# The last residual through TensorE, root and reciprocal on ScalarE and VectorE, and the last scale in three pieces, at the end of a one-core decoder layer

## The chip, the cores and the metric

The kernel runs on one core of a Trainium2 chip. The metric is the device time in microseconds (us). Names of engines: PE is TensorE, DVE is VectorE, ACT is ScalarE, POOL is GpSimd, SP is SyncE, which issues transfers. SBUF is the core's working memory of 128 partitions; PSUM is the memory into which PE writes its sums.

## The reference, cut to what matters

One decoder layer on 256 rows of width 1024, all in fp32. Two branches (block-sparse attention and gated linear attention) are merged by gates; the merged rows go through an output product, are added to the input, and a final normalisation follows:

```
merged = sigmoid(ga + b_merge[0]) * ya + sigmoid(gb + b_merge[1]) * yb
x = x + einsum('bsd,de->bse', merged, w_out)
return rms_norm(x, norm_f_g)

def rms_norm(x, g):
    y = x * rsqrt(mean(x * x, axis=-1) + 1e-6)
    return y * g
```

The change touches only the last two lines: the residual, the mean square, its inverse root, and the scale.

## The kernel before, in words

A number of fp32 precision is made of two numbers of PE's fast type, a high part and a low part, and each product is made of three matmuls: high by high, high by low, low by high (`three`). Weights come in chunks of 512 KB by transfers that SP issues (`load_to`); ACT makes the high part of a chunk (line 179), DVE the low part (line 180), both ahead of PE by a ring of five buffers (`split_to`, `prefetch`). Side work (attention, gates, merging) is written as generators that are stepped on between PE's matmuls by a modelled clock. Each engine works its instructions off in the order in which the code is written; an instruction waits for semaphores of what it reads, and all behind it on its engine wait with it.

The output product (`out_mm`) is the last use of PE. Rows are two tiles t = 0, 1 of 128. Tile 0 has two groups of 512 columns, tile 1 one of 512 and two of 256 (`cuts`); each group sums in a PSUM bank of its own (`po`). First all groups get the lower half of the inner dimension (`half` 0), then, in the order of tiles, the upper half. So the groups end one after the other: (0, 0), (0, 512), (1, 0), (1, 512), (1, 768), where the second number is the first column.

Behind each group stands its epilogue: line 859, DVE adds the input rows `xt` to the bank, into `y`; line 860, ACT squares `y` and sums along the row into a column of `fss` (the square writes a scratch tile, and a second small instruction reads the accumulator out); `scaled` (line 847), DVE multiplies `y` with the gain `nfb` into `yn`; lines 849 and 851, DVE adds the part sum to the mean square plus epsilon in the column `frs`. When a tile's last group is through, POOL raises `frs` to the power -0.5 (line 864), then DVE scales the upper 512 columns of `yn` (line 865) and ACT the lower 512 (line 866), and two transfers of 128 rows of 2 KB each go out: the upper half by SP's queue (line 867), the lower half by ACT's (line 868). In the trace `yn` and `nfb` carry the name `late`, the tile in which they lie, and the scratch tile is `junk`. After the last transfer has landed come the closing steps of the program.

Of the kernel before, what the change touches and what calls it, by code (L numbers as in the profile page):

```python
# [10 lines left out]
F32 = mybir.dt.float32  # L11
F32R = mybir.dt.float32r
BF16 = mybir.dt.bfloat16
I32 = mybir.dt.int32
AF = mybir.ActivationFunctionType
OP = mybir.AluOpType
# [3 lines left out]
P = 128  # L20
S = 256
NT = S // P
D = 1024
KD = D // P
H = 8
DH = 64
HP = H // 2
# [51 lines left out]
def layer(ctx, tc, x, norm_in_g, w_in, b_merge, w_fg2, b_fg, gla_g, w_pa, w_pb, w_out, norm_f_g,  # L79
          rope, causal, sums, masks, out):  # L80
    nc = tc.nc
    one = ctx.enter_context(tc.tile_pool(name="one", bufs=1))
# [7 lines left out]
    def mm(out, lhsT, rhs, start, stop):  # L90
        nc.tensor.matmul(out, lhsT, rhs, start=start, stop=stop)  # L91
        n = out.free_size() / 2400
        clock[0] += n if rhs.dtype == F32R else 4 * n
# [5 lines left out]
    def f32(ap):  # L99
        return ap.bitcast(F32)  # L100
# [4 lines left out]
    def bank(name, tag="acc", bufs=3):  # L105
        return psum.tile([P, 512], F32, name=name, tag=tag, bufs=bufs)

    def small(name):
        return bank(name, "small", 4)
# [73 lines left out]
    def prefetch(i):  # L183

        load_to(i + SPLIT + RAW - 2)
        split_to(i + SPLIT - 1)
# [3 lines left out]
    xt = one.tile([P, NT, D], F32, name="xt")  # L190
# [32 lines left out]
    ones = one.tile([P, P], F32, name="ones")  # L223
    nc.vector.memset(ones, 1.0)
    mhalf = one.tile([P, 4], F32, name="mhalf")
    nc.vector.memset(mhalf, -0.5)
    start = one.tile([P, 1], F32, name="start")
    nc.scalar.activation(start, mhalf[:, :1], AF.Sigmoid)
    ident = one.tile([P, P], F32, name="ident")
# [34 lines left out]
    junk = one.tile([P, D], F32, name="junk", tag="m0")  # L264
# [22 lines left out]
    ggz = one.tile([P, NT, 512], F32, name="ggz")  # L287
    gqT = one.tile([P, 2, S], F32, name="gqT")
    gkT = one.tile([P, 2, S], F32, name="gkT")
    oah = one.tile([P, HP, S], F32R, name="oah")  # L290
    oal = one.tile([P, HP, S], F32R, name="oal")
    obh = one.tile([P, GH, S], F32R, name="obh")
    obl = one.tile([P, GH, S], F32R, name="obl")
# [360 lines left out]
    def tick():  # L654
        step()
        ask = company["ask"]
        if ask and (sum(a[0] for a in ask) >= COMPANY or clock[0] - min(a[1] for a in ask) >= PATIENCE):
            company["open"] = True
            step()
            company["open"] = False  # L660
# [5 lines left out]
    def wait_for(*names):  # L666
        while not all(n in ready for n in names):
            wait(0.3)
# [50 lines left out]
    def three(o, ah, al, bh, bl, first, last):  # L719
        mm(o, ah, bh, start=first, stop=False)  # L720
        mm(o, ah, bl, start=False, stop=False)
        mm(o, al, bh, start=False, stop=last)

    for g in groups:
        ids, name = g["ids"], g["name"]
        if g["kind"] == "K":
            ps = [small(f"{name}{f}") for f in range(3)] + [bank(f"{name}3", "side", 1)]
            for i in ids:
                c = chunks[i]
                k = c["k0"]  # L730
# [13 lines left out]
        elif g["kind"] == "G":  # L744
            ps = {(t, b): (small if t and b else bank)(f"{name}{t}{b}") for t in range(NT) for b in range(2)}
            for i in ids:
                prefetch(i)
                c = chunks[i]
                for kk in range(c["nk"]):
                    k = c["k0"] + kk  # L750
# [8 lines left out]
        elif g["kind"] == "T":  # L759
            ps = [bank(f"{name}{t}") for t in range(NT)]  # L760
            for i in ids:
                prefetch(i)
                c = chunks[i]
                for kk in range(c["nk"]):
                    k = c["k0"] + kk
# [6 lines left out]
        elif g["kind"] == "F":  # L772
# [6 lines left out]
            if name == "gb0":  # L779
# [3 lines left out]
                nfb = late[:, 1, :D]  # L783
# [10 lines left out]
            for b in range(len(ids) // per):  # L794
                i = ids[b * per]
                ps = bank(name) if name != "gqk" else None
                if name == "gqk":
                    for _ in take("small"):
                        wait(0.3)
                    ps = small(name)  # L800
# [14 lines left out]


    def out_mm(ps, t, c0, c1, half):
        for k in range(4 * half, 4 * half + 4):
            c = chunks[oids[c0 // 512, k // 2]]
            ts = slice(t * P, (t + 1) * P)  # L820
            cs = slice(c0 % 512, c0 % 512 + c1 - c0)
            three(ps, merged[0][:, k, ts], merged[1][:, k, ts], c["hi"][:, k % 2, cs], c["lo"][:, k % 2, cs],
                  k == 0, k == KD - 1)

    y = one.tile([P, NT, D], F32, name="y", tag="m0")
    yn = late[:, 0].rearrange("p (t d) -> p t d", d=D)
    junk = work.tile([P, 512], F32, name="junk2", tag="t512", bufs=4)
    fss = one.tile([P, NT, 4], F32, name="fss")
    frs = one.tile([P, NT], F32, name="frs")
    cuts = {(0, 0): [(0, 512)], (0, 1): [(512, 1024)], (1, 0): [(0, 512)], (1, 1): [(512, 768), (768, 1024)]}  # L830
    po = {}
    for n in range(2):
        if n == 0:
            wait_for("m0", "m2")
        for t in range(NT):
            for c0, c1 in cuts[t, n]:
                for i in range(oids[n, 0], oids[n, 0] + 2):
                    prefetch(i)
                tick()
                b = len(po)  # L840
                po[t, c0] = (bank(f"po{b}") if b < 3 else small(f"po{b}"))[:, :c1 - c0]
                out_mm(po[t, c0], t, c0, c1, 0)
    prefetch(len(chunks))
    wait_for("m4", "m6")
    def scaled(t, j, part):
        cs = slice(*part)
        nc.vector.tensor_mul(yn[:, t, cs], y[:, t, cs], nfb[:, cs])
        if j == 0:
            nc.vector.tensor_scalar(frs[:, t:t + 1], fss[:, t, :1], 1.0 / D, EPS, op0=OP.mult, op1=OP.add)
        else:  # L850
            nc.vector.scalar_tensor_tensor(frs[:, t:t + 1], fss[:, t, j:j + 1], 1.0 / D, frs[:, t:t + 1],
                                           op0=OP.mult, op1=OP.add)

    for t in range(NT):
        parts = cuts[t, 0] + cuts[t, 1]
        for j, (c0, c1) in enumerate(parts):
            out_mm(po[t, c0], t, c0, c1, 1)
            cs = slice(c0, c1)
            nc.vector.tensor_add(y[:, t, cs], po[t, c0], xt[:, t, cs])
            nc.scalar.activation(junk[:, :c1 - c0], y[:, t, cs], AF.Square, accum_out=fss[:, t, j:j + 1])  # L860
            if j:
                scaled(t, j - 1, parts[j - 1])
        scaled(t, len(parts) - 1, parts[-1])
        nc.gpsimd.tensor_tensor(frs[:, t:t + 1], frs[:, t:t + 1], mhalf[:, :1], op=OP.pow)
        nc.vector.tensor_scalar(yn[:, t, 512:], yn[:, t, 512:], frs[:, t:t + 1], None, op0=OP.mult)
        nc.scalar.activation(yn[:, t, :512], yn[:, t, :512], AF.Copy, scale=frs[:, t:t + 1])
        nc.sync.dma_start(out[t * P:(t + 1) * P, 512:], yn[:, t, 512:])
        nc.scalar.dma_start(out[t * P:(t + 1) * P, :512], yn[:, t, :512])


_INS = ["x", "norm_in_g", "w_in", "b_merge", "w_gla_fg2", "b_gla_fg", "gla_norm_g", "w_proj_a", "w_proj_b",
# [29 lines left out]
```

## Time and profile before

| | |
|---|---|
| time, median of three runs | 211.7 us (210.26, 211.94, 211.7) |
| the profiled execution | 209.73 us, its span 208.0 us, granted clock of PE 0.997 |
| PE busy | 198.8 us, 96% of the span, 1683 matmuls |
| DVE, ACT, POOL busy | 141.6 (68%), 122.6 (59%), 32.5 (16%) us |
| chain that ended last | PE 67%, DVE 11%, ACT 11%, issue 5%, DMA 2% |

The span runs from the first to the last instruction; the time takes in what lies around it. A share of busy time is a mean over stages; what bounds a stage is read from its timeline and from the chain of work that ended last. PE's matmuls are pipelined, and their recorded lengths overlap.

### The profile page before, as it was taken

The numbers are of one execution on the slowest core, as the hardware profiler recorded it, in microseconds if no ns is written. First come the engines' busy times: TensorE is split into PE (matmuls) and PEld (weight loads), VectorE is DVE, ScalarE is ACT, GpSimd is POOL, SyncE is SP. The second block draws the span as 40 slices with busy tenths as digits, with TensorE's granted clock in tenths as the row PEclk, the third lists the DMA queues.
The fourth block names the chain that finished last, engine by engine and source line by source line (L and its number), as shares of the span: only waits on it lengthen the run. The fifth ranks groups of instructions, "written<-read, shape, count | busy, mean of one in ns | idle before, by whom it ended". The sixth has DMA issues, their size and how long they took to land.

```text
span 208.0 us, 4231 instructions
## 1 busy us (share of the span) xinstructions
PE 198.8 (96%) x1683; PEld 182.4 (88%) x1683; DVE 141.6 (68%) x261; ACT 122.6 (59%) x205; POOL 32.5 (16%) x31
## 2 busy tenths in 40 slices
PE   7999999999999999998999999999999999999970
PEld 2899999899999988775789999999999999989870
DVE  1566778969545899989765556945393959755371
ACT  4369927871999984156775629846455554552251
POOL 2000025800214540103000000200010060420011
PEclk9999999999999999999999999999999999999998
DMA  5999896594364456660343563966344584600022
GB/s 144 349 379 323 238 310 211 135 296 149 101 199 117 145 158 191 193 218 14 107 123 86 182 193 114 294 210 198 108 151 154 168 301 135 204 4 2 0 101 101
DMA packets 28501, 35.39 MB, mean 170 GB/s; under 512 B 1305, under 2 KB 21442, under 8 KB 28482
## 3 DMA queue, kind: packets, MB, share of 16 engines
q1 hardware_dynamic: 28178, 34.60, 54.1%
q10 hardware_dynamic: 304, 0.53, 0.7%
q8 instruction: 13, 0.21, 0.4%
q14 instruction: 6, 0.05, 0.1%
HBM read 34.08 MB, written 1.05 MB: 169 GB/s over the span
## 4 chain that ended last, share of the span: by engine, by line
PE 67%; DVE 11%; ACT 11%; issue 5%; DMA 2%; SPq 1%; POOLq 0%; POOL 0%; ACTq 0%; DVEq 0%
PE ga L91 11%; PE gb L91 11%; PE po L91 8%; PE gg L91 6%; PE gqk L91 6%; PE pa L91 5%; PE pb L91 5%; DVE lo L180 4%; ACT hi L179 4%; PE mg L91 3%; ACT z L700 3%; PE mq L91 3%; DMA xt<-in_x_dram 2%; PE gv L91 2%; DVE EX L417 2%
## 5 line engine op out<-in xcount | busy, mean ns | idle before, releaser
L180 DVE TENSOR_TENSOR lo<-raw,hi 128x1024 fp32r<-128x1024 f32 (+1 forms) x56 | 70.4, 1269 | 23.5 <-ACT hi L179 23.5
L179 ACT CAST hi<-raw 128x1024 fp32r<-128x1024 f32 (+1 forms) x56 | 57.7, 1048 | 21.5 <-PE po L91 6.0
L91 PE MATMUL ga<-xh,hi 128*128 128x256 f32 x64 | 18.1, 283 | 0.0
L91 PE MATMUL gb<-xh,hi 128*128 128x256 f32 x64 | 18.1, 282 | 0.0
L91 PE MATMUL gb<-xh,lo 128*128 128x256 f32 x64 | 17.9, 279 | 0.0
L91 PE MATMUL gb<-xl,hi 128*128 128x256 f32 x64 | 17.9, 279 | 0.0
L91 PE MATMUL ga<-xh,lo 128*128 128x256 f32 x64 | 17.8, 278 | 0.0
L91 PE MATMUL ga<-xl,hi 128*128 128x256 f32 x64 | 17.8, 278 | 0.0
L91 PE MATMUL po<-hi,ml 128*128 128x512 f32 (+1 forms) x40 | 13.9, 347 | 0.0
L91 PE MATMUL po<-lo,mh 128*128 128x512 f32 (+1 forms) x40 | 13.8, 346 | 0.0
L91 PE MATMUL po<-hi,mh 128*128 128x512 f32 (+1 forms) x40 | 13.7, 343 | 0.0
L91 PEld LDWEIGHTS ga<-xh,hi 128*128 128x128 f32 x64 | 12.1, 189 | 0.5 <-issue 0.5
L558 ACT ACTIVATE sm<-sm,mx 128x128 f32<-128x128 f32 (+1 forms) x16 | 7.1, 444 | 8.7 <-DVE mx L553 8.6
L91 PEld LDWEIGHTS gb<-xh,lo 128*128 128x128 f32 x64 | 12.1, 189 | 0.0
L91 PEld LDWEIGHTS gb<-xh,hi 128*128 128x128 f32 x64 | 12.1, 189 | 0.0
L91 PEld LDWEIGHTS ga<-xl,hi 128*128 128x128 f32 x64 | 12.0, 188 | 0.0
L91 PEld LDWEIGHTS gb<-xl,hi 128*128 128x128 f32 x64 | 12.0, 188 | 0.0
L91 PEld LDWEIGHTS ga<-xh,lo 128*128 128x128 f32 x64 | 12.0, 188 | 0.0
L511 POOL TENSOR_TENSOR s<-s,mhalf 128x4 f32<-128x4 f32 x2 | 2.3, 1172 | 54.6 <-DVE s L510 54.6
L624 POOL TENSOR_TENSOR m<-m,sa 128x512 f32<-128x512 f32 x4 | 7.0, 1743 | 23.9 <-DVE m L622 22.0
L91 PE MATMUL mg<-xh,hi 128*128 128x256 f32 x32 | 10.3, 321 | 0.0
L91 PE MATMUL mg<-xl,hi 128*128 128x256 f32 x32 | 9.5, 296 | 0.0
(197 smaller groups left out, 605.7 us busy)
## 6 DMA issues: line engine op xcount, KB each, us to landing
raw<-in_w_in_dram SPq DMA_DIRECT2D x36, 512.0 KB, 3.7
raw<-in_w_out_dram SPq DMA_DIRECT2D x8, 512.0 KB, 4.8
raw<-in_w_in_dram SPq DMA_DIRECT2D x4, 528.0 KB, 6.0
first<-in_w_in_dram SPq DMA_DIRECT2D x8, 256.0 KB, 5.5
raw<-in_w_proj_a_dram SPq DMA_DIRECT2D x4, 512.0 KB, 3.5
raw<-in_w_proj_b_dram SPq DMA_DIRECT2D x4, 512.0 KB, 4.4
xt<-in_x_dram SPq DMA_DIRECT2D x3, 256.0 KB, 5.7
late<-in_norm_f_g_dram SPq DMA_DIRECT2D x1, 512.0 KB, 5.0
```

Of the source, the lines that this page charges most:

```text
L91: nc.tensor.matmul(out, lhsT, rhs, start=start, stop=stop)
L179: nc.scalar.copy(c["hi"], raw)
L180: nc.vector.tensor_sub(c["lo"], raw, f32(c["hi"]))
L417: nc.vector.tensor_mul(e, e, halves(src, LEVELS[l], which))
L511: nc.gpsimd.tensor_tensor(s4, s4, mhalf, op=OP.pow)
L558: nc.scalar.activation(sm[i][:, cs], sm[i][:, cs], AF.Exp, bias=mx[:, i, t:t + 1], scale=0.125, accum_out=den[:, i, t:t + 1])
L624: nc.gpsimd.tensor_add(m, m, cut(sg["ga"]))
L700: nc.scalar.copy(z[i:i + 32], p2[i ^ 32:(i ^ 32) + 32])
```

## The change

The last group, (1, 768), gets its input rows on PE: an identity matrix, and high and low part of `xt` of these columns, are written by DVE into a tile `resid` (which takes the place of a tile whose use is over), and two matmuls with the identity as weights start the group's sum in PSUM. Its square and its scale read the bank itself. The mean square of all groups but the last is kept in `frs`; the last part sum, that column as a bias and the root are one ACT instruction, followed by a reciprocal on DVE. A square root of a column of ones stands ahead of the epilogues. The last scale of a tile is in three pieces: ACT the columns 0 to 255, DVE 768 to 1023 and then 256 to 767; for group (1, 768) the multiplication with the gain and the scale are one DVE instruction. Three transfers go out per tile in place of two, of 128, 128 and 256 KB. Of the memory layout, `part` and an unused tile `gap2` move the tiles allotted after them by 128 bytes per partition.

```diff
     def out_mm(ps, t, c0, c1, half):
+        add = (t, c0) == last
+        if add and not half:
+            mm(ps, resid[:, :P], resid[:, P:3 * P], start=True, stop=False)
+            mm(ps, resid[:, :P], resid[:, 3 * P:], start=False, stop=False)
...
-                  k == 0, k == KD - 1)
+                  k == 0 and not add, k == KD - 1)
...
+    last = (1, 768)
+    resid = one.tile([P, 5 * P], F32R, name="resid", tag="oah")
+    nc.vector.tensor_copy(resid[:, :P], ident)
+    nc.vector.tensor_copy(resid[:, P:3 * P], xt[:, 1, 768:])
+    nc.vector.tensor_sub(resid[:, 3 * P:], xt[:, 1, 768:], f32(resid[:, P:3 * P]))
...
+    part = one.tile([P, NT], F32, name="part")
+    one.tile([P, 24], F32, name="gap2")
+    nc.scalar.activation(start, ones[:, :1], AF.Sqrt)
...
-            nc.vector.tensor_add(y[:, t, cs], po[t, c0], xt[:, t, cs])
-            nc.scalar.activation(junk[:, :c1 - c0], y[:, t, cs], AF.Square, accum_out=fss[:, t, j:j + 1])
+            if (t, c0) == last:
+                z = po[t, c0]
+            else:
+                z = y[:, t, cs]
+                nc.vector.tensor_add(z, po[t, c0], xt[:, t, cs])
+            nc.scalar.activation(junk[:, :c1 - c0], z, AF.Square, accum_out=fss[:, t, j:j + 1])
             if j:
-                scaled(t, j - 1, parts[j - 1])
-        scaled(t, len(parts) - 1, parts[-1])
-        nc.gpsimd.tensor_tensor(frs[:, t:t + 1], frs[:, t:t + 1], mhalf[:, :1], op=OP.pow)
-        nc.vector.tensor_scalar(yn[:, t, 512:], yn[:, t, 512:], frs[:, t:t + 1], None, op0=OP.mult)
-        nc.scalar.activation(yn[:, t, :512], yn[:, t, :512], AF.Copy, scale=frs[:, t:t + 1])
-        nc.sync.dma_start(out[t * P:(t + 1) * P, 512:], yn[:, t, 512:])
-        nc.scalar.dma_start(out[t * P:(t + 1) * P, :512], yn[:, t, :512])
+                mean(t, j - 1)
+            if j == len(parts) - 1:
+                nc.scalar.activation(part[:, t:t + 1], fss[:, t, j:j + 1], AF.Sqrt, bias=frs[:, t:t + 1],
+                                     scale=1.0 / D)
+            if (t, c0) != last:
+                nc.vector.tensor_mul(yn[:, t, cs], z, nfb[:, cs])
+        r = frs[:, t:t + 1]
+        nc.vector.reciprocal(r, part[:, t:t + 1])
+        nc.scalar.activation(yn[:, t, :CUT], yn[:, t, :CUT], AF.Copy, scale=r)
+        for c0, c1 in ((768, D), (CUT, 768)):
+            if (t, c0) == last:
+                nc.vector.scalar_tensor_tensor(yn[:, t, c0:c1], z, r, nfb[:, c0:c1], op0=OP.mult, op1=OP.mult)
+            else:
+                nc.vector.tensor_scalar(yn[:, t, c0:c1], yn[:, t, c0:c1], r, None, op0=OP.mult)
+            nc.sync.dma_start(out[t * P:(t + 1) * P, c0:c1], yn[:, t, c0:c1])
+        nc.scalar.dma_start(out[t * P:(t + 1) * P, :CUT], yn[:, t, :CUT])
```

`CUT` is 256; `mean` holds the two statements that stood in `scaled` behind its multiplication.

The end of DVE's program before, from the add of the last group on (`po_2375` is its bank):

```order
L859 TENSOR_TENSOR y<-po_2375,xt 128x256
L847 TENSOR_TENSOR late<-y,late 128x256
L851 SCALAR_TENSOR_TENSOR frs<-fss,frs 128x1
L847 TENSOR_TENSOR late<-y,late 128x256
L851 SCALAR_TENSOR_TENSOR frs<-fss,frs 128x1
L865 TENSOR_SCALAR late<-late,frs 128x512
```

And of the change, from the add of the group before it on (`po_2379` is now the bank of the last group):

```order
L877 TENSOR_TENSOR y<-po_2366,xt 128x256
L862 TENSOR_SCALAR frs<-fss 128x1
L885 TENSOR_TENSOR late<-y,late 128x256
L864 SCALAR_TENSOR_TENSOR frs<-fss,frs 128x1
L887 RECIPROCAL frs<-part 128x1
L891 SCALAR_TENSOR_TENSOR late<-po_2379,frs,late 128x256
L893 TENSOR_SCALAR late<-late,frs 128x512
```

The add of the last group and its multiplication with the gain are gone; the reciprocal and the fused scale stand behind the last use of `fss`.

The end of ACT's program before, from the transfer of tile 0 on:

```order
L868 DMA out_dram<-late 128x512
L860 ACTIVATE junk_2295,fss<-y 128x512
L860 ACTIVATE junk_2295,fss<-y 128x256 x2
L866 ACTIVATE late<-late,frs 128x512
L868 DMA out_dram<-late 128x512
```

And of the change, from the same place on:

```order
L895 DMA out_dram<-late 128x256
L878 ACTIVATE junk_2295,fss<-y 128x512
L878 ACTIVATE junk_2295,fss<-y 128x256
L878 ACTIVATE junk_2295,fss<-po_2379 128x256
L882 ACTIVATE part<-fss,frs 128x1
L888 ACTIVATE late<-late,frs 128x256
L895 DMA out_dram<-late 128x256
```

The last square reads the bank, and the root stands between it and ACT's scale, which is half as wide.

## Rows read from the trace of the kernel before

**Rows 1.** Chain that ended last: start us, length us, what, how many.
```profile
174.34 5.44 PE pb L91 x48
179.78 16.47 PE po L91 x84
```
**Rows 2.** Timeline, PE's last matmul: start us, length us, engine, line, operation, shapes.
```profile
201.43 0.28 PE L91 MATMUL po<-hi,ml 128*128 128x256 f32 x1
```
**Rows 3.** Timeline behind it; in brackets idle time before and its releaser; q: queue.
```profile
201.74 0.42 DVE L859 TENSOR_TENSOR y<-po,xt 128x256 f32<-128x256 f32 x1 [0.28 <-PE po L91]
202.08 0.41 DVE L847 TENSOR_TENSOR late<-y,late 128x256 f32<-128x256 f32 x1
202.26 0.42 ACT L860 ACTIVATE junk<-y 128x256 f32<-128x256 f32 x1 [0.84 <-DVE y L859]
...
202.58 0.19 ACT L860 ACTIVATION_READ_ACCUMULATOR junk<-y 128x1 f32 x1
202.82 0.15 DVE L851 SCALAR_TENSOR_TENSOR frs<-fss,frs 128x1 f32<-128x1 f32 x1
203.05 0.56 POOL L864 TENSOR_TENSOR frs<-frs,mhalf 128x1 f32<-128x1 f32 x1 [4.11 <-DVE frs L851]
203.64 0.72 ACT L866 ACTIVATE late<-late,frs 128x512 f32<-128x512 f32 x1 [0.87 <-POOL frs L864]
203.65 0.49 DVE L865 TENSOR_SCALAR late<-late,frs 128x512 f32<-128x512 f32 x1 [0.67 <-POOL frs L864]
204.16 0.36 SPq L867 DMA_DIRECT2D out_dram<-late  x1
204.40 0.34 ACTq L868 DMA_DIRECT2D out_dram<-late  x1
```
**Rows 4.** Windows: stretch, us, busy by engine (count), PE clock, DMA share, GB/s.
```profile
204.16:205.00 0.84, 0.00 (x0) 0.00 (x0) 0.00 (x0) 0.21 (x1) 0.00 (x0) 1.00 0.00 0
205.00:206.40 1.40, 0.00 (x0) 0.00 (x0) 0.00 (x0) 0.00 (x0) 0.00 (x0) 1.00 0.99 370
```
**Rows 5.** Transfers: target, queue, count, KB each, median us from issue to landing.
```profile
out_dram<-late SPq DMA_DIRECT2D x2, 256.0 KB, 2.1
out_dram<-late ACTq DMA_DIRECT2D x2, 256.0 KB, 2.5
```
**Rows 6.** Timeline, idle stretches of DVE and ACT ahead of the epilogues.
```profile
185.02 1.23 DVE L180 TENSOR_TENSOR lo<-raw,hi 128x1024 fp32r<-128x1024 f32 x1 [2.40 <-ACT hi L179]
...
194.25 0.63 ACT L860 ACTIVATE junk<-y 128x512 f32<-128x512 f32 x1 [3.10 <-DVE y L859]
```
**Rows 7.** Groups of instructions: line, engine, form, count; busy us, mean ns; idle before.
```profile
L386 ACT ACT_TABLE_LOAD x1 | 1.3, 1283 | 0.0
L507 ACT ACTIVATE sq<-o 128x512 f32<-128x512 f32 x2 | 1.2, 598 | 5.9 <-PE o L91 5.9
L228 ACT ACTIVATE start<-mhalf 128x1 f32<-128x1 f32 x1 | 0.2, 202 | 0.0
L257 DVE SCALAR_TENSOR_TENSOR xl<-xp,vecs,xh 128x256 fp32r<-128x256 f32 x8 | 3.9, 482 | 3.4 <-ACT xh L256 3.4
```
**Rows 8.** Timeline, tile 0's last square and tile 1's first two adds.
```profile
197.06 0.63 ACT L860 ACTIVATE junk<-y 128x512 f32<-128x512 f32 x1 [2.08 <-DVE y L859]
...
199.37 0.68 DVE L859 TENSOR_TENSOR y<-po,xt 128x512 f32<-128x512 f32 x1
...
200.38 0.42 DVE L859 TENSOR_TENSOR y<-po,xt 128x256 f32<-128x256 f32 x1 [0.32 <-PE po L91]
```
**Rows 9.** Timeline of DVE, a reciprocal and the scale that reads it.
```profile
91.15 0.17 DVE L562 RECIPROCAL den<-den 128x2 f32<-128x2 f32 x1 [0.31 <-ACT sm L558]
91.36 0.28 DVE L564 TENSOR_SCALAR sm<-sm,den 128x128 f32<-128x128 f32 x1
```
**Rows 10.** Windows, a stretch with weight loads in rows of 1 KB.
```profile
145.00:150.00 5.00, 5.00 (x47) 5.00 (x46) 1.41 (x2) 2.44 (x4) 0.00 (x0) 1.00 0.47 149
```
**Rows 11.** GB/s in 40 equal slices of the span; the first weights' transfers.
```profile
GB/s 144 349 379 323 238 310 211 135 296 149 101 199 117 145 158 191 193 218 14 107 123 86 182 193 114 294 210 198 108 151 154 168 301 135 204 4 2 0 101 101
...
first<-in_w_in_dram SPq DMA_DIRECT2D x8, 256.0 KB, 5.5
```

More of the change, by code (lines that the diff above doesn't have):

```diff
@@ L289, in layer @@
     gkT = one.tile([P, 2, S], F32, name="gkT")
-    oah = one.tile([P, HP, S], F32R, name="oah")
+    oah = one.tile([P, HP, S], F32R, name="oah", tag="oah")
     oal = one.tile([P, HP, S], F32R, name="oal")
@@ L844, in layer, with mean @@
     wait_for("m4", "m6")
-    def scaled(t, j, part):
-        cs = slice(*part)
-        nc.vector.tensor_mul(yn[:, t, cs], y[:, t, cs], nfb[:, cs])
+    part = one.tile([P, NT], F32, name="part")
+    one.tile([P, 24], F32, name="gap2")
+    nc.scalar.activation(start, ones[:, :1], AF.Sqrt)
+    def mean(t, j):
         if j == 0:
@@ L852, in scaled @@
                                            op0=OP.mult, op1=OP.add)
+    CUT = 256
     for t in range(NT):
```

## Prediction

> **What bounds the kernel now.** First I read the chain that ended last. Nearly all of it is TensorE (PE): the output product alone stands in it as one unbroken piece of 84 matmuls, 16.47 us [rows 1]. So PE sets the time up to its last instruction, and no work that another engine does beside it is worth anything. Then I read the timeline behind the last matmul. The last of them starts at 201.43 and lasts 0.28 us [rows 2]; VectorE (DVE) takes up PE's result at 201.74. From here no PE is left, and one step follows the other [rows 3]: residual add on DVE (201.74), square with sum on ScalarE (ACT, 202.26), reading of its accumulator (202.58, done at 202.77), two small DVE steps of which the second (202.82) adds the last part sum, the power on GpSimd (POOL, 203.05, 0.56 us long), then the last scale, half on ACT and half on DVE (203.64), and two output transfers of 256 KB, issued by SyncE's queue at 204.16 and by ACT's at 204.40. Between the result of PE and the two issues lie 2.42 and 2.66 us.
>
> The windows behind the issues say what the transfers wait for [rows 4]: up to 205.00 no byte moves, from 205.00 to 206.40 the sixteen DMA engines are full (share 0.99, 370 GB/s). 370 GB/s over 1.40 us is 518,000 bytes, all but 1% of the 512 KB. The two transfers thus share one full pipe: its end is set by when the first of them was issued (204.16 + 0.84 = 205.00) and by the bytes, as long as the second arrives before the first has drained. They land 2.1 and 2.5 us after issue [rows 5], the second at 206.9; 1.1 us of closing steps follow to the end of the span at 208.0. The profiled execution took 209.73 us, 1.73 more than its span. The three timed runs lie at 210.26 to 211.94 with median 211.7; the profiled one is thus 0.9% below the median, and I carry the difference that I work out over to the median.
>
> **The change part by part.**
>
> *Residual through PE.* Two matmuls of 128x256 are added, ahead of the end of PE's queue, and PE is the bound: 48 of this size took 5.44 us [rows 1], 0.113 each, so all behind comes 0.23 us later. If they did not overlap as their neighbours do, it would be 2 x 0.28 = 0.56 [rows 2]. I take 0.23, since they are of the same type and width as their neighbours. Gone is the DVE add: from 201.74 to the square at 202.26 are 0.52 us [rows 3].
>
> *The preparation of the residual* is three DVE instructions (two casts, one subtraction), put ahead of weight splits (the low parts of the last weights). Each is no wider than the add of 128x256, 0.42 us [rows 3]; together at most 1.3 us. DVE stood idle for 2.40 us before the split at 185.02 [rows 6], and PE's unbroken piece runs past that, so the delay ends there and I cost it at nothing; without that idle time a weight split would come 1.3 us later.
>
> *The root's table.* A table load (1283 ns for those in the trace [rows 7]) and a square root of one column are put on ACT where it sat idle for 3.10 us, up to 194.25 [rows 6]: 1.28 + 0.2 fits, so nothing. The order of instructions has no further load behind it.
>
> *The new path behind PE* (PE's result now at 201.74 + 0.23 = 201.97):
> - square directly from PSUM: the accumulator was read 0.32 after the square began [rows 3]; ACT's square out of PSUM took 0.60 us where that out of SBUF took 0.63 [rows 7, 8], so 0.30 (at most 0.33). Reading 0.19: 202.46.
> - root with the sum of the earlier parts as its bias: it waits for its own engine. DVE's reciprocal and the scale that reads it start 0.21 apart at a length of 0.17 [rows 9], so such a wait costs 0.04. The root itself: no row. The nearest is the one-column activation with 202 ns [rows 7]; a column operand adds about 0.09, as the 0.72 us of the scale against the 0.63 of the square show [rows 3, 8]. I take 0.29, with 0.20 as the lower end: 202.79.
> - hand over to DVE 0.05 (202.77 to 202.82 [rows 3]), reciprocal and its wait 0.21 [rows 9]: 203.05. In place of this stood the add of the part sum, the pass to POOL, 0.56 us of power and the pass back, 202.77 to 203.64 = 0.87 [rows 3]. The new way from 202.46 to 203.05 takes 0.59.
> - DVE's fused scale of 256 columns out of PSUM: 482 ns for this form [rows 7], between 0.42 (the add) and 0.50: 203.53, issued on SyncE's queue 0.02 later at **203.55**. The scale of the other 512 columns starts 0.40 after it (0.08 of overlap, as between DVE's instructions before), takes 0.49 [rows 3]: 203.94, issue at **203.96**; the queue is free by then (an issue takes 0.36).
> - ACT's scale of 256 columns in place of 512: starts with DVE's at 203.05, 0.42 + 0.09 = 0.51, issue at **203.60**.
>
> *The transfers.* Three in place of two, same bytes. First byte 0.84 after the first issue, 204.39; the two pieces of 128 KB last 0.70 at 370 GB/s, to 205.09; the third can start at 203.96 + 0.84 = 204.80, so the pipe never runs dry and all ends at 204.39 + 1.40 = 205.79, against 206.40. That is **0.61 us** earlier, which is just the shift of the first issue (204.16 to 203.55). If instead the last transfer's own duration counts, the shift of the last issue decides: 204.40 - 203.96 = 0.44. The trace has the pipe at 0.99 share and both transfers of a tile inside one stretch, so I take 0.61.
>
> The Trainium skill puts this otherwise: its page "DMA: Bandwidth & Descriptors", section "Anatomy of one DMA", fits each DMA as about 2.0 us plus bytes over 436 GB/s, and the section "Measured" tells to batch to 1 MiB or more, which speaks against cutting 512 KB in three. By that fit a piece of 256 KB takes 2.6 us by itself (an estimate), and the gain would be 0.44. The trace has 2.1 and 2.5 for two that run together, so the fixed part is there, but it overlaps.
>
> *Tile 0's tail* gets the same edits and lies beside PE's matmuls of tile 1. Its square starts at 197.06 [rows 8], now 0.23 later: accumulator 197.83 to 198.02, root done at 198.35, reciprocal and wait 198.61, two scales at most 0.40 apart each: 199.41, when the add of tile 1 can start. It started at 199.37, and the next add waited 0.32 for PE [rows 8]: 0.04 late, hidden. The part sum that the last root needs as bias is ready some 0.1 to 0.3 us before its square begins; the root itself comes 0.5 later.
>
> **Sum.** 209.73 - 0.61 = 209.12 for an execution like the profiled one; 211.7 - 0.61 = **211.1** for the median. By the ends of the terms: earlier by 0.15 (root at 0.20, fused scale at 0.42) gives 0.76; later (0.33 more on PE, 0.03 on the square, 0.02 on the fused scale) gives 0.23.
>
> **Rivals.**
> - *The pieces give it back.* Rows of 1 KB in place of 2 KB could move more slowly. A stretch that loads weights in rows of 1 KB moved 149 GB/s at a share of 0.47, 317 per full pipe [rows 10]. At that rate for 256 KB the pipe lasts 0.12 longer; at half the rate 0.70 longer, and the gain is gone: 211.7. Against it: the pipe here is limited by its engines, and rows of 1 KB filled them at 86% of the rate.
> - *Slower: the transfers of one queue follow one another.* SyncE's queue now has two of the last three. If the second started only when the first had landed, the issue at 203.55 lands at 205.65, and 2.1 later, at 207.75, the other: 0.85 later than 206.9, so 212.5. It decides as soon as a wait of more than 0.6 us stands between the two. Against it: the first weights, in transfers of 256 KB on this same queue, took 5.5 us each to land, 48 GB/s if one had followed the other, and the second and third of the 40 slices of that time moved 349 and 379 GB/s [rows 11].
> - *The change does nothing for the end*, because the exit (1.1 us of closing steps) waits for something else. Against it: the second landing, at 206.9 [rows 5], is the last thing that any engine but the exit shows. It would give 211.7.
> - *More than worked out:* the pass over POOL costs more in other executions than the 0.87 us of the profiled one. No row tells; 1 us more of it gives 210.1.
>
> **How the numbers follow.** Forecast (0.2 to 0.8 us gained): 0.68. Pieces or exit take it back, within 0.2 of before: 0.18. One queue serial, or another new wait in the tail: 0.06. More than 0.8 gained: 0.08. The forecast's own range is 210.9 to 211.5. The timed runs spread over 1.68 us, though, and a median of a few of them moves by about half of that whatever the kernel, so the range goes on both sides beyond that: 209.7 is a gain of 0.8 taken from 210.5, which lies a third of the way up among the four times of the kernel before (209.73 to 211.94), and 212.0 is the gain gone and 0.3 of spread. About 1% (2.1 us) is what a measurement of this kernel can tell from no change. No case reaches 1% by its mechanism: faster takes the spread and the gain together, 0.07; slower the serial queue and the spread, 0.03; within, 0.90.
>
> **What would show it.** In the profile after: PE's last matmul about 0.23 later; ACT's last square starting directly behind PE, no add; root, reciprocal and fused scale inside 1.6 us; three issues near 203.55, 203.60 and 203.96; DMA full from 204.4 to 205.8; span near 207.4. Wrong if the table load stands in the tail, if the DMA windows show a gap or a lower rate at full share, if a split of weights now holds PE near 185 to 195, or if the closing 1.1 us grow.

## The result, and the profile after

The changed kernel takes 211.14 us (median of 20 runs, 210.44 to 213.11), the kernel before 209.79 us in runs between them on the same chip (20 runs, 209.12 to 212.03). The ratio is 1.0061, with a 95% interval of [1.0041, 1.0081]: **0.6% or 1.3 us slower, where 0.3% faster was forecast.** The three runs that the forecast started from had their median 1.9 us above that of the 20, so that the forecast of 211.1 lies beside the measured 211.14 by accident. What counts is the difference, and it has the other sign.

The profiled execution took 211.15 us, its span is 209.4 us; before it was 209.73 and 208.0. The 1.4 us are split by one moment, the start of PE's last matmul:

| | before | after | difference | forecast |
|---|---|---|---|---|
| start of PE's last matmul, us | 201.43 | 203.66 | +2.23 | +0.23 |
| from there to the end of the span, us | 6.53 | 5.71 | -0.82 | -0.84 |
| span, us | 207.96 | 209.37 | +1.41 | -0.61 |

The end behind PE went nearly as worked out, 0.82 less against 0.84. The two added matmuls take some of it back: with the 0.23 of the forecast 0.59 are gained, with the 0.3 that they cost in the runs below 0.5, against 0.61. But PE came to its end 2.0 us later than two more matmuls explain.

The timeline of after behind PE's last matmul (start us, length us, engine, line, operation; in brackets the idle time before and its releaser; q is a queue), which answers to [rows 2, 3]:

```profile
203.66 0.28 PE L91 MATMUL po<-hi,ml 128*128 128x256 f32 x1
...
204.03 0.38 ACT L878 ACTIVATE junk<-po 128x256 f32<-128x256 f32 x1 [0.39 <-PE po L91]
204.31 0.19 ACT L878 ACTIVATION_READ_ACCUMULATOR junk<-po 128x1 f32 x1
204.54 0.29 ACT L882 ACTIVATE part<-fss,frs 128x1 f32<-128x1 f32 x1
204.87 0.16 DVE L887 RECIPROCAL frs<-part 128x1 f32<-128x1 f32 x1 [1.03 <-ACT part L882]
205.06 0.51 ACT L888 ACTIVATE late<-late,frs 128x256 f32<-128x256 f32 x1 [0.23 <-DVE frs L887]
205.07 0.48 DVE L891 SCALAR_TENSOR_TENSOR late<-po,frs,late 128x256 f32<-128x256 f32 x1
205.47 0.48 DVE L893 TENSOR_SCALAR late<-late,frs 128x512 f32<-128x512 f32 x1
205.58 0.33 SPq L894 DMA_DIRECT2D out_dram<-late  x1
205.60 0.35 ACTq L895 DMA_DIRECT2D out_dram<-late  x1
```

Each step stands where the forecast had put it, counted from the last matmul: the square directly behind PE, root, reciprocal and fused scale, the first issue on SyncE's queue at 205.58, 1.92 behind the matmul (forecast: 203.55 - 201.66 = 1.89). The windows behind that issue (stretch, us, busy time by engine and count, PE's clock, DMA share, GB/s) answer to [rows 4], and the transfers (queue, count, KB, median us from issue to landing) to [rows 5]:

```profile
205.58:206.42 0.84, 0.00 (x0) 0.00 (x0) 0.36 (x1) 0.00 (x0) 0.00 (x0) 1.00 0.01 5
206.42:207.82 1.40, 0.00 (x0) 0.00 (x0) 0.00 (x0) 0.00 (x0) 0.00 (x0) 0.71 1.01 358
```
```profile
out_dram<-late SPq DMA_DIRECT2D x2, 256.0 KB, 2.4
...
out_dram<-late SPq DMA_DIRECT2D x2, 128.0 KB, 1.9
out_dram<-late ACTq DMA_DIRECT2D x2, 128.0 KB, 2.2
```

0.84 us without bytes, then 1.40 us of full DMA engines, as before. At about the same share three transfers move 358 GB/s where two moved 370: the lower rate at full share that the prediction named as a sign against it is there, but it is 3%, and from the first issue to the end of the span it is 3.79 us as against 3.80 before.

So the loss lies ahead. The chain that ended last in after (start us, length us, what, how many) answers to [rows 1]:

```profile
158.78 5.66 PE pa L91 x48
164.44 5.65 PE pb L91 x48
...
181.39 22.56 PE po L91 x122
```

48 matmuls of `pb` take 5.65 us where the same product took 5.44. The windows over the four stretches of `pa` and `pb`, 192 matmuls (the counts take in one or two at the edges), before and then after, show what else is different:

```profile
158.00:179.78 21.78, 21.78 (x194) 21.78 (x193) 16.96 (x20) 11.56 (x15) 4.62 (x3) 1.00 0.58 186
```
```profile
158.78:181.39 22.61, 22.61 (x193) 22.61 (x193) 18.18 (x22) 11.64 (x15) 3.89 (x3) 1.00 0.58 178
```

The same matmuls, PE busy without a gap in both, its granted clock 1.00 in both, and 0.83 us more. None of the changed instructions runs here but the preparation of the residual, from 179.86 on. PE is not waiting for anybody: its matmuls follow one another more slowly. PE's timeline shows it one by one, before and then after:

```profile
139.63 0.28 PE L91 MATMUL gb<-xh,hi 128*128 128x256 f32 x1
139.74 0.28 PE L91 MATMUL gb<-xl,hi 128*128 128x256 f32 x1
```
```profile
139.66 0.28 PE L91 MATMUL gb<-xh,lo 128*128 128x256 f32 x1
139.78 0.28 PE L91 MATMUL gb<-xh,hi 128*128 128x256 f32 x1
```

Worked out over whole stretches, the starts lie 113.3 ns apart (5.44 us / 48) or 117.8 ns (5.65 / 48). Whole stretches keep one pace or the other. In before, about 440 matmuls of 256 columns stand at 113 ns and 540 at 118; in after, 76 and 921. The two traces part early: comparing the same matmul in both, after is 0.25 us late at 85 us; a wait for another engine takes this in (at 90 to 107 us the two are level); then it is 0.5 late at 124, 0.8 at 157, 1.6 at 179, 2.2 at the end. The only thing in the change that can reach back to 85 us is where the tiles lie: `part` and `gap2` push the ring of weight chunks (`raw`, `hi`, `lo`) and the work tiles 128 bytes further in each partition. Nothing that these matmuls read beside `hi` and `lo` (`xh`, `xl`, `oah` to `obl`, the merged rows) has moved.

### The profile page after: what moved, and what is told of

Its sections match the earlier page's. It is cut to its first block, busy times and chain, and to the rows that moved or that the text cites. A ratio compares the mean times of both kernels' runs of the same rounds, so it can differ in the third digit from the quotient of the medians.

```text
span 209.4 us, 4245 instructions
## 1 busy us (share of the span) xinstructions
PE 201.4 (96%) x1685; PEld 184.2 (88%) x1685; DVE 144.7 (69%) x264; ACT 124.1 (59%) x209; POOL 35.2 (17%) x29
## 4 chain that ended last, share of the span: by engine, by line
PE 89%; DVE 3%; ACT 2%; DMA 2%; SPq 1%; issue 1%; DVEq 0%; ACTq 0%
PE ga L91 11%; PE gb L91 11%; PE po L91 11%; PE gg L91 6%; PE gqk L91 5%; PE mk L91 5%; PE pa L91 5%; PE mq L91 5%; PE pb L91 5%; PE mv L91 5%; PE gv L91 5%; PE mg L91 3%; DMA xt<-in_x_dram 2%; PE pv L91 2%; PE a L91 1%; PE o L91 1%
## 5 line engine op out<-in xcount | busy, mean ns | idle before, releaser
L180 DVE TENSOR_TENSOR lo<-raw,hi 128x1024 fp32r<-128x1024 f32 (+1 forms) x56 | 71.4, 1288 | 23.1 <-ACT hi L179 23.1
L704 POOL TENSOR_TENSOR kT<-kT,z 128x512 f32<-128x512 f32 x2 | 10.4, 5216 | 7.2 <-DVE z L703 7.2
L624 POOL TENSOR_TENSOR m<-m,sa 128x512 f32<-128x512 f32 x4 | 5.2, 1310 | 26.9 <-DVE m L622 23.6
```

Of the source, the lines that this page charges most:

```text
L180: nc.vector.tensor_sub(c["lo"], raw, f32(c["hi"]))
L624: nc.gpsimd.tensor_add(m, m, cut(sg["ga"]))
L704: nc.gpsimd.tensor_add(dst, dst, z)
```

## The experiments

The theory: the placement of `hi` and `lo` sets PE's pace, and costs about 2 us; the edits of the tail gain 0.6. The rival: the new code itself costs PE's pace (another order of instructions, table load, more work for DVE), and the placement is nothing. Every kernel here computes the whole reference. Ratios are to the kernel before, run in turn on the same chip.

One figure of the traces serves for all of them: PE's way, the time from the start of its first matmul of `gg` to the start of its last. In before it runs from 20.45 to 201.43 us, 180.97; in after from 20.38 to 203.66, 183.28. What lies ahead of it, where PE still waits for the first transfers, scatters: in the sixteen profiled executions PE's way starts between 19.6 and 22.2 us.

**The shift alone, and the change without it.** The kernel before with one unused tile, allotted where the change allots `part` and `gap2`:

```diff
     wait_for("m4", "m6")
+    one.tile([P, 32], F32, name="shift")
```

> The kernel before with one unused tile of 128 bytes per partition behind the fixed tiles, so that raw, hi, lo and all work tiles lie 128 bytes further on, as in the changed kernel; no instruction differs. If the place of these buffers sets PE's pace (theory layout), most stretches of 256-column matmuls run at 0.118 us each as in the changed kernel, and the time is about 2 us (1%) above before. If the pace has another cause (theory program: two more matmuls, more instructions on the queues, or chance per execution), the time is that of before within 0.3%.

And the changed kernel with a tile whose use is over in place of `part`, so that nothing moves:

```diff
-    part = one.tile([P, NT], F32, name="part")
-    one.tile([P, 24], F32, name="gap2")
+    part = ss[:, :, 0]
```

> The changed kernel without its tiles part and gap2: the root is written into a column of ss, which is no longer read, so every buffer lies where it lay before. Layout: PE's pace is that of before, only the tail differs, and the time is 0.5 to 0.7 us (0.3%) below before. Program: 1 to 1.4 us above before, as the changed kernel.

Measured: the shift alone 211.84 us, ratio 1.0095 [1.0069, 1.0122]; the change without it 209.24 us, 0.9967 [0.9948, 0.9987]. The chains, of the shift alone and of the change without the shift:

```profile
159.52 5.66 PE pa L91 x48
```
```profile
157.94 5.46 PE pa L91 x48
163.40 5.44 PE pb L91 x48
```

The first and the last matmul of the change without the shift (e2_noshift):

```profile
20.40 0.28 PE L91 MATMUL gg<-hi,xh 128*128 128x256 f32 x1
...
201.67 0.28 PE L91 MATMUL po<-hi,ml 128*128 128x256 f32 x1
```

An unused tile turns the old code to the wide pace (49 matmuls at 113 ns, 943 at 118; PE's way 182.98 us in place of 180.97), and the new code without it keeps the old pattern (416 and 570 against 441 and 540; PE's way 181.27, of which 0.3 are the two added matmuls). So the loss comes with the tile and without the new code, and the rival falls. The sum also closes: 0.33% gained by the edits (0.7 us, with an interval of 0.3 to 1.1) and 0.95% lost by the shift (2.0 us) make +1.3 us, which is the measured change.

**Which tiles.** The kernel before again, with the pad behind the ring (only work tiles move), ahead of `hi` (`raw` stays), or between `hi` and `lo`. In the last two the work tiles, which lie behind the ring, move too. Each run has one of the three additions; the brackets name it.

```diff
+            if done[0] == 0:
+                ring.tile([P, 32], F32, name="shift", bufs=1)   (e5_hilo: ahead of hi)
             hi = ring.tile([P, SMAX], F32R, name="hi", bufs=SPLIT)
+            if done[0] == 0:
+                ring.tile([P, 32], F32, name="shift", bufs=1)   (e6_lo: ahead of lo)
             lo = ring.tile([P, SMAX], F32R, name="lo", bufs=SPLIT)
...
     wait_for("m4", "m6")
+    ring.tile([P, 32], F32, name="shift", bufs=1)   (e4_work: behind the ring)
```

> The kernel before with the unused tile of 128 bytes behind the ring buffers: raw, hi and lo stay, the work tiles (sm, ob, z, m and the like) move by 128 bytes. If hi and lo, PE's weights, are what counts, the time is that of before within 0.3%; if the work tiles count, about 2 us above; theory program expects that of before as well.

> The kernel before with the unused tile of 128 bytes between the raw and the split buffers: raw stays, hi and lo (and the work tiles, which did not count in the run before) move by 128 bytes. If it is the place of PE's operands that sets the pace (theory weights), the time is about 1% above before, as with all buffers moved, and the 256-column matmuls stand 0.118 us apart. If it is the place of raw, which only ACT, DVE and the transfers touch (theory raw), the time is that of before within 0.3%.

> The kernel before with the unused tile between hi and lo: hi and raw stay, lo moves by 128 bytes. Theory weights, each operand for itself: two of three matmuls read hi and one lo, so between 0 and 1% above before, 0.3% if the cost goes by the count. If hi alone, or the place of lo against hi, counts, it ends near 0 or near 1% or above. Theory raw: that of before.

Work tiles alone: 210.03 us, ratio 0.9994 [0.9965, 1.0023], no difference that the times show. In the trace there is one: PE's way is 181.47 us, 0.50 longer than before, since two stretches that were close are wide, first in before, then in e4_work:

```profile
107.26 7.02 PE ga L91 x60
...
116.53 7.50 PE ga L91 x66
```
```profile
107.31 7.26 PE ga L91 x60
...
116.83 7.78 PE ga L91 x66
```

In these stretches PE reads no work tile, and their chunks and rows lie where they lay. `hi` and `lo` (and the work tiles) with `raw` in its place: 211.93 us, 1.0102 [1.0069, 1.0136], PE's way 182.92, the whole loss. `lo` and the work tiles: 209.22 us, 0.999 [0.9958, 1.0023], no difference that the medians show; its ten runs spread from 208.41 to 211.24. But PE's way is 180.01 us, 0.96 shorter than before, with some 830 matmuls 112 to 115 ns apart (444 in before). So, with all else at the same place, `hi` costs (e5_hilo against e6_lo), and `lo` gains on PE (e6_lo against e4_work).

**How far.** The changed kernel with other sizes of the pad: without `gap2` (a shift of 32 bytes), with 8 floats (64) and with 56 floats (256):

```diff
-    one.tile([P, 24], F32, name="gap2")
+    one.tile([P, 56], F32, name="gap2")
```

> The changed kernel without gap2: part alone moves the buffers by 32 bytes. Layout: a time that differs from the changed kernel's (1.006 of before), in which direction is open; program: 1.006 of before again.

> The changed kernel with gap2 smaller: all buffers 64 bytes further on than before. With the period of 256 this is a place not seen yet (0, 32 and 128 gave 0.997, 1.012 and 1.006): a time between 0.995 and 1.015 of before. If what counts is only whether the address is 32 past a multiple of 64, as in the kernel before, the value of the run with 0 would not differ from that with 128, so I expect near 1.006 or above.

> The changed kernel with gap2 larger, so that all buffers lie 256 bytes further on than before in place of 128. If the pace goes by the address within 256 bytes (theory weights with that period), it is that of the run without a shift: 0.997 of before, 1% below the changed kernel. If any move from the place of before costs, or the period is longer, 1.006 of before or more.

| shift of `hi` and `lo`, bytes | 0 | 32 | 64 | 128 | 256 |
|---|---|---|---|---|---|
| time, us | 209.24 | 212.47 | 212.69 | 211.14 | 208.98 |
| ratio | 0.9967 | 1.0120 | 1.0136 | 1.0061 | 0.9971 |
| interval | [0.9948, 0.9987] | [1.0095, 1.0145] | [1.0103, 1.0170] | [1.0041, 1.0081] | [0.9945, 0.9997] |
| PE's way, us | 181.27 | 184.02 | 184.22 | 183.28 | 181.27 |

The chain of the kernel with 64 bytes:

```profile
160.47 5.70 PE pa L91 x48
```

At 32 and 64 bytes the pace is wider still, 119 ns (5.70 / 48). At 256 bytes the time, PE's way and the pattern (413 at 113 ns, 566 at 118) are those of no shift. More bytes are not worse; the place within 256 bytes is what the results follow, as far as one full period can tell.

**Absolute place or distance.** The change without its shift, and an earlier pad (`gap0`, allotted at line 242, ahead of `xh` and `xl`) made 128 bytes longer, which moves `hi`, `lo` and the operands that PE reads with them (`xh`, `xl`, `oah` to `obl`, and `mh`, `ml`, the merged rows, which lie where `xh` and `xl` were) by the same amount:

```diff
-    one.tile([P, 8], F32, name="gap0")
+    one.tile([P, 40], F32, name="gap0")
```

> The changed kernel, root in ss, with the unused tile ahead of xh 128 bytes larger: both operands of PE, weights' parts hi and lo and activations' parts (xh, xl, oah and the rest), move by 128 bytes together, so their distance is that of before. If PE's pace goes by the distance between the two operands that it reads at once, 0.997 of before, as without a shift. If it goes by the place of hi and lo alone, 1.003 to 1.006, as in the changed kernel.

209.06 us, ratio 0.998 [0.9944, 1.0016], PE's way 181.22 us, 452 matmuls at 113 ns and 520 at 118, from `gg` on in the same stretches as without the shift. The chain has the close pace again:

```profile
158.84 5.46 PE pa L91 x48
```

So it is no address by itself, but where tiles lie to one another. With the work tiles worth 0.50 us and `raw` nothing (PE's way is 182.98 us where it moves along, 182.92 where it does not), the weight chunk and the rows, which a matmul reads together, are the pair that this points at. It can't be their distance alone: e4_work made two stretches wide and left it as it was.

**`hi` and `lo` apart.** The change without its shift and `lo` moved by 128 bytes (as in e6_lo), and the same with `hi` moved by 128 and `lo` by 256 (both pads of the diff above, so that within 256 bytes `lo` is where it was). The work tiles, behind `lo`, move with it by 128 and by 256:

> The changed kernel with hi and raw where they lay before and lo 128 bytes further on. With lo there the kernel before had its last matmul at 200.28 us in place of 201.43 in its profile, and 0.999 [0.996, 1.002] of its time. If that shorter PE stretch is repeatable and the tail's gain adds to it, 0.993 of before (208.0 to 208.5 us); if the stretch was one execution's luck, 0.996 to 0.997, the value without a shift.

> The changed kernel, root in ss (no shift of the fixed tiles), hi 128 bytes and lo 256 bytes further on than before: within 256 bytes the places of hi and lo are exchanged against the run with lo moved (0.991 of before). If what counts is that hi and lo lie 128 apart within 256, the time is 0.99 of before again. If each has its own good place (hi at 32, and lo at 160 within 256 bytes), it is the value with both at 160 or worse: 1.004 to 1.01.

The first takes 208.10 us, ratio 0.9914 [0.9895, 0.9933], and beats both kernels; 834 matmuls at 113 ns, 120 at 118. The second takes 210.66 us, 1.0035 [0.9992, 1.0078], its ten runs from 209.49 to 212.51; the profiled one took 212.13 and started PE's way late, at 22.20 in place of 20.40. Their chains, first e9_lo_change and then e13_swap:

```profile
131.51 5.44 PE gb L91 x48
...
161.49 5.44 PE pb L91 x48
```
```profile
135.46 5.71 PE gb L91 x48
...
166.06 5.44 PE pb L91 x48
```

Put beside each other, with the moves within 256 bytes, ratio and PE's way in us:

| | `lo`, work tiles +0 | `lo`, work tiles +128 |
|---|---|---|
| `hi` +0 | 0.9967 (181.27) | 0.9914 (180.37) |
| `hi` +128 | 1.0035 (182.45) | 1.0061 (183.28) |

In the two cases where only one of them is moved, upper right and lower left, `hi` and `lo` are 128 bytes further apart or nearer, which within 256 is the same; one is the best of all and the other behind the kernel without a shift. So the distance of `hi` from `lo` alone does not decide. `hi`, which two of three matmuls read, costs when it is moved, wherever `lo` is, but not in the same stretches nor by the same amount: 1.2 us of PE's way with `lo` in its place, where `pa` and `pb` stay close (5.44 in the chain), and 2.9 with `lo` moved too, where they are wide. `lo` gains where `hi` stays, 0.90 us of PE's way here and 0.96 in the kernel before (e6_lo), and costs 0.83 where `hi` moves; in the times the gain stands clear of noise only here.

**The parts of the tail, on the change without its shift.** Two pieces and two transfers instead of three:

```diff
-    CUT = 256
+    CUT = 512
...
-            nc.sync.dma_start(out[t * P:(t + 1) * P, c0:c1], yn[:, t, c0:c1])
+        nc.sync.dma_start(out[t * P:(t + 1) * P, CUT:], yn[:, t, CUT:])
```

> The changed kernel without a shift and with the last scale in two pieces of 512 columns and two transfers, as before. From the last matmul to the end of the span (5.7 us with three pieces) the prediction's terms give +0.26: DVE's fused 256 columns at 203.05 of its clock, then 256 more at 203.45, done at 203.80, issue 0.27 later than the first issue of three pieces. If cutting the transfers costs what it saves (rival: pieces give it back), +0.0.

The residual added by DVE again:

```diff
-    last = (1, 768)
+    last = None
```

> The changed kernel without a shift and with the last residual added by DVE again, so two matmuls fewer, no fused scale, root and three pieces kept. The terms give: PE's last matmul 0.23 earlier; from it to the end 0.52 longer for the add, 0.03 for a square from SBUF, 0.1 to 0.2 shorter for a plain scale from SBUF: 6.1 in place of 5.7 us, so the end 0.1 to 0.2 later. If PE waits for the residual's preparation or takes longer for the two matmuls than 0.23, the end comes earlier.

The power on POOL again, without table load, root and reciprocal:

```diff
-                nc.scalar.activation(part[:, t:t + 1], fss[:, t, j:j + 1], AF.Sqrt, bias=frs[:, t:t + 1],
-                                     scale=1.0 / D)
+                mean(t, j)
...
-        nc.vector.reciprocal(r, part[:, t:t + 1])
+        nc.gpsimd.tensor_tensor(r, r, mhalf[:, :1], op=OP.pow)
```

> The changed kernel without a shift and with the power on POOL again in place of root and reciprocal (the last part sum added by DVE first, as before; no table load). The terms give 0.87 from the end of the accumulator's reading to the scales in place of 0.59: +0.28, so 6.0 us from the last matmul to the end. If the root chain is no shorter than the power, 5.7.

| | time, us | ratio | last matmul to end of span, us | against 5.71 |
|---|---|---|---|---|
| e2_noshift | 209.24 | 0.9967 [0.9948, 0.9987] | 5.71 | |
| e10_two_pieces | 209.44 | 0.9986 [0.9967, 1.0004] | 6.08 | +0.37 |
| e11_dve_add | 208.94 | 0.9942 [0.9920, 0.9964] | 6.07 | +0.36, last matmul 0.25 earlier: +0.11 |
| e12_pow | 209.97 | 0.9985 [0.9964, 1.0007] | 6.31 | +0.60 |

In time none of the three stands clear of e2_noshift, all intervals overlap; what a part is worth is read from one profiled execution each. PE's way tells that they differ behind PE alone: 181.28 and 181.27 us in e10_two_pieces and e12_pow against 181.27, and 180.99 in e11_dve_add, two matmuls fewer. These matmuls thus cost 0.28 (forecast 0.23).

Their timelines behind PE, first of e10_two_pieces, whose last matmul starts at 201.24:

```profile
203.40 0.35 ACTq L894 DMA_DIRECT2D out_dram<-late  x1
203.42 0.36 SPq L893 DMA_DIRECT2D out_dram<-late  x1
```

The first issue comes 2.16 behind the last matmul in place of 1.92: that is 0.24 of the 0.37. The span ends 3.92 behind this issue in place of 3.79, the other 0.13, for a reason that no row here shows. An early first issue is what the third piece buys.

Of e11_dve_add (last matmul 201.42):

```profile
202.25 0.42 ACT L873 ACTIVATE junk<-y 128x256 f32<-128x256 f32 x1 [0.85 <-DVE frs L859]
...
203.70 0.33 SPq L889 DMA_DIRECT2D out_dram<-late  x1
```

The square starts 0.83 behind the last matmul, with the residual on PE 0.37: 0.46 gained. The first issue is only 0.36 later, since the first piece is now scaled from SBUF and is shorter than the fused scale out of PSUM; and 0.25 to 0.28 goes to PE. In all some 0.1 is left, and the two ratios overlap: this part of the change buys nothing that these runs can measure.

Of e12_pow (last matmul 201.91):

```profile
202.34 0.19 ACT L876 ACTIVATION_READ_ACCUMULATOR junk<-y 128x1 f32 x1
202.56 0.38 ACT L876 ACTIVATE junk<-po 128x256 f32<-128x256 f32 x1
...
203.31 0.56 POOL L884 TENSOR_TENSOR frs<-frs,mhalf 128x1 f32<-128x1 f32 x1 [3.83 <-DVE frs L862]
203.90 0.51 ACT L885 ACTIVATE late<-late,frs 128x256 f32<-128x256 f32 x1 [0.86 <-POOL frs L884]
```

The last square starts 0.65 behind the matmul in place of 0.37: ACT is still at the square before it, 0.28 late. The rest of the 0.60, some 0.32, is the way over POOL. The expectation, 0.28, had only this second part.

## Why the prediction was wrong

**The step that failed: PE's pace was carried over unchanged.** The prediction's sum has for PE one term, "48 of this size took 5.44 us [rows 1], 0.113 each, so all behind comes 0.23 us later". It took 5.44 as a property of the matmul, and PE's time up to the two new ones as unchanged. It is one of two paces, and both stand in the trace of before; its chain has, ahead of [rows 1], the same count in

```profile
132.99 5.66 PE gb L91 x48
```

at 117.9 ns each, which the prediction never set beside the 5.44. The shift by 128 bytes was known from the diff and named ahead of the prediction as part of the change, and the kernel has two unused tiles of its own around `xh` and `xl` (`gap0` and `gap1`, lines 242 and 245), but it got no term, no bound and no rival. It is worth 2.0 us (1.0095 with the shift alone, and 1.0061 / 0.9967 = 1.0094 with it and without it in the new code): three times all that the tail gains. That nothing changes ahead of the first changed instruction was a silent assumption; an edit of the memory layout acts on every instruction that uses a moved tile. The chances followed from that: slower had been given only to a serial queue and to the spread.

*The chain was read too far.* "Nearly all of it is TensorE" does not hold: PE has 67% of it, and the piece of 84 matmuls ends at 196.25, where the chain goes over to tile 0's epilogue and POOL. Behind that stands

```profile
198.38 0.56 POOL frs L864
198.94 4.08 issue
```

That PE bounds the end all the same is shown by the timeline instead, in which PE's last matmul releases DVE's add [rows 2, 3].

**What was right.** *The tail:* 0.5 to 0.6 net against 0.61, with the square at +0.37 behind the last matmul (forecast 0.31), the root at 0.88 (0.84), the scale at 1.41 (1.39), the first issue at 1.92 (1.89). The root with a bias column took 0.29 as estimated, the fused scale 0.48, the scale of 256 columns on ACT 0.51, reciprocal and wait 0.20. *The transfers:* counted from the last matmul, the end came 0.82 earlier, the first issue 0.81 and the last one (206.01 in place of 204.40) only 0.62, so the end moved with the first; three pieces fill the pipe without a gap, at 358 GB/s. The fit and the rule that the prediction takes from the Trainium skill's page "DMA: Bandwidth & Descriptors" are stated there for transfers that GpSimd issues; these go out by SyncE's and ACT's queues. *The root's table:* hidden; from ACT's timeline of after,

```profile
193.20 1.28 ACT L857 ACT_TABLE_LOAD   x1
194.50 0.20 ACT L857 ACTIVATE start<-ones 128x1 f32<-128x1 f32 x1
196.37 0.63 ACT L878 ACTIVATE junk<-y 128x512 f32<-128x512 f32 x1 [1.67 <-DVE y L877]
```

1.67 us were left over. *The change without its shift:* 0.7 us gained (0.3 to 1.1), where 0.61 was worked out.

**What was right with a wrong size.** The preparation of the residual was bounded at 1.3 us and took 1.79 (179.86 to 181.65, when the next split starts). The subtraction alone took 1.41 where at most 0.42 had been put, beside an instruction of POOL, which the bound had left out. From DVE's and POOL's timelines of after:

```profile
180.09 1.35 POOL L624 TENSOR_TENSOR m<-m,sa 128x512 f32<-128x512 f32 x1 [7.49 <-DVE m L622]
```
```profile
180.31 1.41 DVE L841 TENSOR_TENSOR resid<-xt,resid 128x256 fp32r<-128x256 f32 x1
181.65 2.35 DVE L180 TENSOR_TENSOR lo<-raw,hi 128x1024 fp32r<-128x1024 f32 x2
...
186.72 1.23 DVE L180 TENSOR_TENSOR lo<-raw,hi 128x1024 fp32r<-128x1024 f32 x1 [2.12 <-ACT hi L179]
```

It is still hidden: DVE idles 2.12 us ahead of the split at 186.72 (2.40 before [rows 6]).

**Rivals.** The pieces give next to nothing back: 358 GB/s in place of 370, and the end as long behind the first issue as before. The queue is not serial: two transfers of SyncE's queue share the one stretch. The exit follows the landing: 3.79 us from the first issue to the end of the span, 3.80 before. The pass over POOL is worth some 0.32 (e12_pow), where 0.28 follows from the prediction's terms. None of the four had anything to do with the loss.

**Left open.** That the layout sets PE's pace is shown: five kernels whose tiles lie alike to one another within 256 bytes (e2_noshift, e7_shift256, e10_two_pieces, e12_pow, e14_all) have a PE's way of 181.22 to 181.28 us, and other layouts of the changed kernel one that is 0.9 shorter to 2.9 longer. By what mechanism, and why of two stretches on the same tiles one is close and one wide, no run here shows. It is not the distance of `hi` from `lo` alone, nor an absolute address, nor the distance of chunk and rows alone; that 256 bytes is the period rests on one pair of kernels.

## What to carry to other kernels

A change of memory layout, an unused tile among it, is an edit of every instruction that reads a moved tile: where one engine runs without a gap for the whole kernel, a shift needs a term of its own, or the experiment that undoes it. First read an engine's pace (time of a stretch over its count) in several stretches of the trace before; two paces for one form at one clock say that something unnamed sets it, and one per cent of the busiest engine outweighs all that this tail gave. To see such an effect, compare the time between the same two instructions of that engine in two traces: here it repeats within 0.06 us where the layout is the same, while the timed runs of one kernel scatter by 1 to 3. Here the best kernel, 208.10 us, is the change without its shift and with `lo` and the work tiles 128 bytes further.

## What the runs showed of the hardware

- TensorE's 128x256 matmuls in this precision stand 113.3, 117.8 or 119 ns apart at a granted clock of 1.00, and how many stand at each pace follows from where tiles lie to one another: with the ring and the work tiles 0, 32, 64, 128 and 256 bytes further the ratios are 0.9967, 1.0120, 1.0136, 1.0061 and 0.9971; with `lo` and the work tiles 128 further, 0.9914; with the rows moved along by 128, 0.998.
- An instruction of DVE with two inputs in SBUF hardly moves on while one of POOL that began before it runs: in after, 1.41 us for at most 0.42, and a split of a weight chunk that starts at 168.31 beside POOL's instruction of 168.18 to 169.47 takes 2.24 in place of 1.23. In before the order is turned round, and it is POOL that loses: the split starts at 167.24 and takes 1.23, POOL's instruction starts at 167.38 and takes 2.24, where the next one takes 1.29. The Trainium skill's page "SBUF — State Buffer", section "Who interferes with whom", says that a DVE instruction with two SBUF inputs contends with a GpSimd instruction that reads SBUF, and that "Issue order, not op shape, decides who blocks." The traces agree in both orders; in after DVE's two instructions end 0.28 and 1.08 us behind POOL's, not far from their lengths when alone.
- Of two or three output transfers that share the pipe, the end goes by the first issue: 0.84 us later the bytes flow, for 1.40 us at 370 GB/s (two) or 358 (three), and the span ends 3.79 to 3.81 us behind that issue in before, after, e11_dve_add and e12_pow, 3.92 in e10_two_pieces.
